# Norms between sub-layers handed on in pieces of 256 columns, and an unread target of squares that orders nothing

## The chip, the core and the metric

The kernel runs on one core of a Trainium2 chip. A core has four engines that compute, each with its own queue of instructions that it works off in order: TensorE (PE, matmuls and transposes into PSUM), VectorE (DVE), ScalarE (ACT) and GpSimd (POOL). A further one, SyncE (SP), issues most DMAs. They meet by semaphores. The metric is the time of one execution in microseconds.

## The reference

A decoder trunk of two layers on 256 tokens of width 1024. Each layer has three sub-layers, and each of these has a root-mean-square norm ahead of it and one behind it, whose output is added to the residual x:

```python
def rms_norm(x, g):
    xf = x.astype(jnp.float32)
    y = xf * lax.rsqrt(jnp.mean(xf * xf, axis=-1, keepdims=True) + RMS_EPS)
    return (y * g.astype(jnp.float32)).astype(x.dtype)
```

The sub-layers are a mix of four token mixers, a cross-attention into 256 memory tokens, and an MLP with squared ReLU of width 4096. All of it is in float32.

## The kernel before, in words

The 256 tokens are two tiles of 128 (t0 and t1), with tokens on partitions. The residual x is kept as two tiles of 128 by 1024. A matmul of float32 quality is made from three (`mm3`): operands are split into a rounded part (hi, cast by ScalarE) and what is left (lo, a VectorE subtraction). Weights are read by DMA into five slots called raw, cast, subtracted and used.

A sub-layer ends with a product of 256 tokens by 1024 (`wide`), which fills two PSUM banks of 512 columns for each token tile, t0 first. Behind it stands a boundary, for each tile the following steps. `post_bank`: ScalarE squares a bank and sums the squares; the squares themselves go to an unread tile named junk; VectorE multiplies the bank by a gain. `post`: GpSimd adds eps to the sum and takes a power, which are two instructions on 128 by 1; VectorE makes the new x from that scale in two halves of 512 columns. `pre`: VectorE multiplies x by the next norm's gain (xg), TensorE transposes xg in two groups of four blocks into banks C, ScalarE copies each group (the rounded part of hT) and VectorE makes the low part. Sums of squares of the new x follow, for a scale that is used later. Where the MLP ends and the next layer's mix begins (`normed`), the scale is needed at once: it is put on a diagonal (g<-ident) and the transposes are matmuls with that diagonal.

The order of instructions on every engine is made at build time by a planner: an operation is ready when what it depends on is planned, ready ones are taken by start time, then rank, then place in the program. Tiles come from pools with few slots (`NB`), PSUM banks from pools A, B, C and S. A pool with one slot makes its users follow one another: the junk tile was such a pool, so that all squares kept the order of the program.

At the start, x is loaded in four DMAs on the queues of SP and ACT, c0 of both tiles and then c1, and `pre_first` scales both tiles on diagonals and fills four banks A with 128-column matmuls, bank by bank for both tiles.

In the trace, L631 is ScalarE's helper, L642, L648 and L654 are VectorE's (L654 GpSimd's too), L676 GpSimd's power, L685 a matmul, L690 a transpose, L728 and L738 DMA issues.

Of the kernel before, what the change touches and what calls it, by code (L numbers as in the profile page):

```python
# [12 lines left out]
BF16 = mybir.dt.bfloat16  # L13
AF = mybir.ActivationFunctionType
OP = mybir.AluOpType
# [4 lines left out]
D = 1024  # L20
T = 256
# [3 lines left out]
C = 64  # L25
RMS_EPS = 1e-6
# [191 lines left out]
def body(nc, tc, wts, x, mem, memT, pc, rows, r256, cmpw, cmpe, relb, lora, cst, out, dbg=None):  # L218
    from contextlib import ExitStack
    with ExitStack() as ctx:  # L220
# [4 lines left out]
        Prog(nc, tc, sb, ps, dr, wts, x, mem, memT, pc, rows, r256, cmpw, cmpe, relb, lora, cst, out, dbg).run()  # L225


NB = {"raw": 5, "hi": 8, "lo": 8, "g8": 7, "g4": 12, "g2": 13, "g1": 5, "junk": 1, "s": 14, "x8": 6,
      "p1": 1, "tok1": 1, "tok2": 1, "lk": 1, "ng": 1}
NPS = {"A": 4, "B": 2, "C": 2, "S": 8}  # L230

# [7 lines left out]
           "sb": ()}  # L239
HOME = {tag: s for s, tags in STRETCH.items() for tag in tags}  # L240
LEAD = 24
KEEP = 1000.0
TICK = 10.24 / 3
WARM = 3060
# [4 lines left out]
class VT:  # L249
# [4 lines left out]
    def __init__(self, name, shape, dtype, tag, dram=False):  # L254
        self.name, self.shape, self.dtype, self.tag, self.dram = name, tuple(shape), dtype, tag, dram
        self.real = None
        self.likes = range(4, 7) if tag == "g8" else ()
# [110 lines left out]
class Sched:  # L368
# [10 lines left out]
    def add(self, eng, cost, outs, ins, emit, cols=0.0):  # L379
        op = Op(eng, cost, [v for v in outs if isinstance(v, V)], [v for v in ins if isinstance(v, V)], emit,  # L380
                self.rank, len(self.ops))
        op.cols = cols
        self.ops.append(op)
        for v in op.ins:
            t = v.t
            for w, box in t.writes:
                if t.psum or meet(box, v.box):
                    self.dep(op, w, LAT[w.eng] if w.eng != eng else OWN[eng])
            t.reads.append((op, v.box))
        for v in op.outs:  # L390
            t = v.t
            for w, box in t.writes:
                if t.psum or meet(box, v.box):
                    self.dep(op, w, 0.0 if w.eng == eng else LAT[w.eng])
            for r, box in t.reads:
                if r is not op and (t.psum or meet(box, v.box)):
                    self.dep(op, r, 0.0 if r.eng == eng else 0.1)
            t.writes.append((op, v.box))
        for v in op.outs + op.ins:
            if not v.t.ops or v.t.ops[-1] is not op:  # L400
                v.t.ops.append(op)
        if eng == "PE" and self.after is not None:
# [204 lines left out]
class Prog:  # L607
# [226 lines left out]
    def setup(self):  # L834
        self.pct = self.keep([128, DEPTH, NPC], "pct")
        self.warm_up()
        xr = self.x.rearrange("o (t p) d -> p (o t) d", p=128)
        self.xt = [self.keep([128, D], "x%d" % t) for t in range(2)]
        for c in range(2):
            for t, eng in enumerate((self.nc.sync, self.nc.scalar)):  # L840
                cs = slice(512 * c, 512 * c + 512)
                self.dma(self.xt[t][:, cs], xr[:, t, cs], eng=eng)
        self.dma(self.pct, self.pc)
        self.ident = self.keep([128, 128], "ident")
        self.s.add("POOL", 0.5, [self.ident], [], lambda: make_identity(self.nc, real(self.ident)))
        self.mhalf = self.keep([128, 8], "mhalf")
        self.memset(self.mhalf, -0.5)

    def warm_up(self):
# [71 lines left out]
    def sumsq(self, src_list):  # L921

        acc = self.small(2)
        for i, s in enumerate(src_list):
            j = self.tile([128, 512], "junk", BF16)
            self.act(j, s, AF.Square, scale=D ** -0.5, accum=acc[:, i:i + 1])
        return acc

# [6 lines left out]
    def to_hT_half(self, t, q, src, hT, scale=None):  # L935


        hh, hl = hT
        p = self.bank("C", (128, 4, 128))
        for j in range(4):  # L940
# [5 lines left out]
        self.split(hh[:, 4 * q:4 * q + 4, s], hl[:, 4 * q:4 * q + 4, s], p)  # L946
# [8 lines left out]
    def pre(self, t, g, hT, normed, out):  # L955


        x = self.xt[t]
        xg = self.tile([128, D], "g4")
        H2 = (slice(0, 512), slice(512, 1024))  # L960

        def stat():
            return self.rstd(self.sumsq([x[:, :512], x[:, 512:]]))

        for s in H2:
            self.tt(xg[:, s], x[:, s], g[:, s], OP.mult)
        scale = None
        if normed:
            scale = self.tile([128, 128], "g1")
            self.ts(scale, self.ident, stat())  # L970
        for q in range(2):
            self.to_hT_half(t, q, xg[:, 512 * q:512 * q + 512], hT, scale)
        if normed is False:
            out[t] = stat()
        elif normed is None:
# [4 lines left out]
            out[t] = e  # L980

    def pre_first(self, hT):
        dg = []
        for t, x in enumerate(self.xt):
            if t == 0:
                acc = self.sumsq([x[:, :512], x[:, 512:]])
            else:
                acc = self.small(2)
                sq = self.tile([128, 512], "g2")
                self.stt(sq, x[:, :512], 1.0 / D, x[:, :512], OP.mult, OP.mult)  # L990
                self.red(acc[:, 0:1], sq, OP.add)
                j = self.tile([128, 512], "junk", BF16)
                self.act(j, x[:, 512:], AF.Square, scale=D ** -0.5, accum=acc[:, 1:2])
            dg.append(self.tile([128, 128], "g1"))
            self.ts(dg[-1], self.ident, self.rstd(acc))
        for q in range(4):
            p = self.bank("A", (128, 2, T))
            for t in range(2):
                for k in range(2):
                    i = 128 * (2 * q + k)  # L1000
                    self.mm(p[:, k, 128 * t:128 * t + 128], self.xt[t][:, i:i + 128], dg[t])
            for k in range(2):
                self.split(hT[0][:, 2 * q + k], hT[1][:, 2 * q + k], p[:, k], self.pcol(0, "g_pre", 1, 2 * q + k))

    def post_bank(self, st, i, bank, g, cs=None):

        if not st:
            st.extend((self.small(4), self.tile([128, D], "g4")))
        acc, yg = st
        cs = cs or slice(512 * i, 512 * i + 512)  # L1010
        j = self.tile([128, 512], "junk", BF16)[:, :cs.stop - cs.start]
# [3 lines left out]
    def post(self, t, st, eps, out=None, after=None):  # L1015

        acc, yg = st
        a, b = acc if isinstance(acc, tuple) else (acc[:, 0:1], acc[:, 1:2])
# [3 lines left out]
        x = self.xt[t]  # L1022
        for i in range(2):
            cs = slice(512 * i, 512 * i + 512)
            op = self.stt(x[:, cs], yg[:, cs], rr, x[:, cs], OP.mult, OP.add)
            if after is not None:
                self.s.dep(op, after, -9.0)
            if out is not None:
                self.dma(out[:, cs], x[:, cs])

    def boundary(self, t, st, eps, gpre, hT, normed, rs):
        self.post(t, st, eps)
        self.pre(t, gpre, hT, normed, rs)

    def at(self, rank, f, *args):
# [5 lines left out]
    def wide(self, l, names, act, gpost, done):  # L1041

        banks = [[self.bank("A") for _ in range(2)] for _ in range(2)]
        ah, al = act
        for half in range(2):
            ks = range(4 * half, 4 * half + 4)
            us = []
            for t in range(2):
# [5 lines left out]
                for k, c in order:  # L1054
# [643 lines left out]
    def mix(self, l, hT):  # L1698
# [69 lines left out]
        self.hT, self.rs = xT, {}  # L1768

        def done(t, st):  # L1770
            self.at(0, self.boundary, t, st, 4 * D * RMS_EPS, gpre, xT, False, self.rs)

        self.wide(l, [("mo", k) for k in range(8)], mT, gpost, done)
        self.dump("x_mix", self.xt)
# [75 lines left out]
    def xattn(self, l):  # L1850
# [384 lines left out]
```

## Time and profile before

| what | value |
|---|---|
| median of 3 runs | 1087.66 us (1087.47 to 1088.67) |
| the profiled execution, its own time | 1090.18 us |
| its span in the trace | 1088.1 us |
| TensorE busy | 1069.9 us |
| VectorE, ScalarE, GpSimd busy | 856.8, 657.5, 96.1 us |

The rows below come from the page's first section and from two views of the trace: the table of stretches, which gives for each engine its busy time in a stretch, and the timeline, which gives the start, the time and the form of instructions on one engine, with the idle time ahead of them and what ended it in brackets.

### The profile page before, as it was taken

The page shows a single profiled execution, that of the slowest core. Times are in us where ns is not written, and L with a number is a line of the kernel's source. Part 1 is how long each engine was busy: PE and PEld are TensorE (multiplying, and loading weights), DVE is VectorE, ACT ScalarE, POOL GpSimd, SP SyncE. Part 2 cuts the span into 40 slices and gives each one's busy share as a digit, 9 for nine tenths or more (in the row PEclk, how much of TensorE's full clock was granted, in tenths as well). Part 3 has the DMA queues.
Part 4 walks back from the last instruction along what each step waited for, and adds up shares of the span by engine and source line. Part 5 has one row for each costly group of instructions (what it writes and reads, how often), then busy time and mean ns, then how long its engine had stood idle before and what let it go on. Part 6 is the DMA issues. An engine that isn't in the chain of part 4 may idle for free.

```text
span 1088.1 us, 20208 instructions
## 1 busy us (share of the span) xinstructions
PE 1069.9 (98%) x7848; PEld 936.1 (86%) x7848; DVE 856.8 (79%) x1347; ACT 657.5 (60%) x1069; POOL 96.1 (9%) x154
## 2 busy tenths in 40 slices
PE   8999999999999999999999999999999999999997
PEld 7989877888998899999889998778888987999996
DVE  6867887866767689888796767977867667999997
ACT  7574655645555667776665664644546455776673
POOL 2000011001100110000020000100002002000000
PEclk9999999999999999999999999999999999999999
DMA  8546555755546699998945257356645467889981
GB/s 328 164 128 183 210 174 165 266 186 169 170 157 218 212 273 288 267 279 254 298 165 172 79 160 254 126 174 201 237 164 173 149 224 210 255 267 293 270 265 51
DMA packets 75970, 225.18 MB, mean 207 GB/s; under 512 B 12223, under 2 KB 14015, under 8 KB 75748
## 3 DMA queue, kind: packets, MB, share of 16 engines
q1 hardware_dynamic: 71268, 207.65, 55.7%
q0 software_dynamic: 4320, 15.73, 8.8%
q8 instruction: 61, 1.00, 0.4%
q10 hardware_dynamic: 288, 0.52, 0.2%
q14 instruction: 33, 0.27, 0.1%
HBM read 221.77 MB, written 3.15 MB: 207 GB/s over the span
## 4 chain that ended last, share of the span: by engine, by line
PE 88%; DMA 3%; DVE 3%; issue 2%; ACT 2%; POOL 2%; SPq 0%; POOLq 0%; DVEq 0%; ACTq 0%
PE A L685 47%; PE C L685 18%; PE S L685 12%; PE B L685 8%; DMA g<-wts 2%; PE C L690 2%; DVE g L642 1%; POOL s L654 1%; DMA raw<-wts 1%; ACT junk L631 1%; DVE lo L642 1%; DVE x L648 1%; ACT g L631 1%; PE B L690 0%; POOL s L676 0%
## 5 line engine op out<-in xcount | busy, mean ns | idle before, releaser
L642 DVE TENSOR_TENSOR lo<-raw,hi 128x1024 fp32r<-128x1024 f32 (+1 forms) x308 | 368.4, 1213 | 70.2 <-ACT hi L631 41.8
L631 ACT ACTIVATE hi<-raw 128x1024 fp32r<-128x1024 f32 (+1 forms) x308 | 316.2, 1049 | 136.7 <-PE A L685 67.1
L685 PE MATMUL A<-hi,g 128*128 128x512 f32 (+2 forms) x1152 | 370.3, 389 | 0.9 <-ACT g L631 0.5
L685 PEld LDWEIGHTS A<-hi,g 128*128 128x128 f32 x1152 | 214.5, 188 | 48.1 <-issue 4.3
L685 PE MATMUL A<-lo,g 128*128 128x512 f32 (+2 forms) x576 | 220.2, 382 | 0.0
L642 DVE TENSOR_TENSOR g<-g,g 128x512 f32<-128x512 f32 (+3 forms) x218 | 187.9, 886 | 9.8 <-ACT g L631 8.5
L631 ACT ACTIVATE g<-g 128x512 fp32r<-128x512 f32 (+7 forms) x228 | 149.0, 693 | 43.3 <-DVE g L642 19.6
L685 PE MATMUL A<-g,hi 128*128 128x256 f32 x928 | 169.2, 285 | 0.0
L685 PE MATMUL C<-g,hi 128*128 128x256 f32 x960 | 167.7, 278 | 1.1 <-ACT g L631 1.1
L685 PEld LDWEIGHTS C<-g,hi 128*128 128x128 f32 x960 | 147.4, 188 | 3.7 <-ACT g L631 1.5
L685 PEld LDWEIGHTS A<-g,hi 128*128 128x128 f32 x928 | 141.2, 188 | 5.2 <-issue 3.4
L685 PE MATMUL C<-g,lo 128*128 128x256 f32 x480 | 133.5, 278 | 0.0
L685 PE MATMUL A<-g,lo 128*128 128x256 f32 x464 | 129.1, 278 | 0.0
L631 ACT ACTIVATE g<-C 128x512 fp32r<-128x512 f32 (+5 forms) x119 | 59.4, 513 | 110.8 <-PE C L685 84.6
L685 PEld LDWEIGHTS A<-lo,g 128*128 128x128 f32 x576 | 108.4, 188 | 17.5
L685 PE MATMUL S<-g,g 128*128 128x512 f32 x450 | 108.3, 391 | 0.3 <-DVE g L642 0.3
L685 PEld LDWEIGHTS S<-g,g 128*128 128x128 f32 x450 | 84.3, 188 | 19.0 <-DVE g L642 0.8
L685 PEld LDWEIGHTS C<-g,lo 128*128 128x128 f32 x480 | 91.0, 190 | 0.0
L685 PEld LDWEIGHTS A<-g,lo 128*128 128x128 f32 x464 | 87.3, 188 | 0.2 <-DVE lo L642 0.2
L631 ACT ACTIVATE g<-A 128x512 f32<-128x512 f32 (+3 forms) x70 | 39.5, 567 | 54.4 <-PE A L685 42.3
L654 POOL TENSOR_SCALAR s<-s 128x1 f32<-128x1 f32 (+1 forms) x38 | 27.3, 719 | 349.8 <-ACT junk L631 297.1
L642 DVE TENSOR_TENSOR g<-C,g 128x512 fp32r<-128x512 f32 (+3 forms) x66 | 37.0, 587 | 23.7 <-ACT g L631 17.3
(144 smaller groups left out, 1079.0 us busy)
## 6 DMA issues: line engine op xcount, KB each, us to landing
raw<-wts SPq DMA_DIRECT2D x300, 512.0 KB, 4.7
g<-wts SPq DMA_DIRECT2D x90, 256.0 KB, 5.3
g<-wts POOLq DMA_DIRECT2D x30, 512.0 KB, 5.7
g<-rows SPq DMA_DIRECT2D x11, 512.0 KB, 4.7
g<-memT SPq DMA_DIRECT2D x12, 256.0 KB, 6.9
g<-cmpw SPq DMA_DIRECT2D x4, 512.0 KB, 4.5
raw<-wts SPq DMA_DIRECT2D x4, 498.0 KB, 6.2
raw<-wts SPq DMA_DIRECT2D x4, 480.0 KB, 6.2
```

Of the source, the lines that this page charges most:

```text
L631: e = lambda: self.nc.scalar.activation(real(out), real(in_), func, bias=real(bias), scale=real(scale), accum_out=real(accum))
L642: f = lambda: e.tensor_tensor(real(out), real(a), real(b), op)
L648: f = lambda: self.nc.vector.scalar_tensor_tensor(real(out), real(a), real(s), real(b), op0=op0, op1=op1)
L654: f = lambda: e.tensor_scalar(real(out), real(a), real(s1), real(s2), op0=op0, **kw)
L685: e = lambda: self.nc.tensor.matmul(real(out), real(lhsT), real(rhs), start=start, stop=stop, skip_group_check=True)
L690: self.pe(0.109, out, [in_, self.ident], lambda: self.nc.tensor.transpose(real(out), real(in_), real(self.ident)), 128)
```

## The change

The junk tile is kept for the whole program, and writes to it make no dependencies (`sink`). At boundaries that aren't `normed`, the new x, xg and the transposes come in pieces of 256, 256 and 512 columns (`PIECES`), `post_bank` and the boundary have rank -1, and the squares of the new x rank 3. The two halves of x of t0 are loaded first, one by each queue, and `pre_first` makes all matmuls of t0 before those of t1.

```diff
-NB = {"raw": 5, "hi": 8, "lo": 8, "g8": 7, "g4": 12, "g2": 13, "g1": 5, "junk": 1, "s": 14, "x8": 6,
+NB = {"raw": 5, "hi": 8, "lo": 8, "g8": 7, "g4": 12, "g2": 13, "g1": 5, "s": 14, "x8": 6,
...
+PIECES = ((0, 2), (2, 2), (4, 4))
...
         for v in op.outs:
             t = v.t
+            if t.sink:
+                continue
...
-        for c in range(2):
-            for t, eng in enumerate((self.nc.sync, self.nc.scalar)):
+        for t in range(2):
+            for c, eng in enumerate((self.nc.sync, self.nc.scalar)):
...
+        self.junk = self.keep([128, 512], "junk", BF16)
+        self.junk.t.sink = True
...
+        for k, n in PIECES:
+            s = slice(128 * k, 128 * (k + n))
+            self.x_new(t, s)
+            self.tt(xg[:, s], x[:, s], g[:, s], OP.mult)
+            self.to_hT(t, k, n, xg[:, s], hT)
+        old = self.rank(3)
         if normed is False:
-            out[t] = stat()
+            out[t] = self.rstd(self.sumsq([x[:, :512], x[:, 512:]]))
...
-        for q in range(4):
-            p = self.bank("A", (128, 2, T))
-            for t in range(2):
+        ps = [self.bank("A", (128, 2, T)) for _ in range(4)]
+        for t in range(2):
+            for q, p in enumerate(ps):
                 for k in range(2):
...
-                        self.post_bank(st, c, banks[t][c], gpost)
+                        self.at(-1, self.post_bank, st, c, banks[t][c], gpost)
...
-            self.at(0, self.boundary, t, st, D * RMS_EPS, gpre, hT, None, self.rs)
+            self.at(-1, self.boundary, t, st, D * RMS_EPS, gpre, hT, None, self.rs)
```

The planner turns this into other orders. At the fourth boundary (cross-attention to MLP, layer 1), TensorE had the eight transposes of t0 (C from xg and ident) in two groups, three matmuls ahead of the end of t1's second bank (A_10267); then came the MLP's first bank (A_10425):

```order
5338 L685 MATMUL A_10267<-hi_10175,g_1916_10000 128x512
5339 L685 MATMUL A_10267<-lo_10241,g_1916_10000 128x512
5340 L685 MATMUL A_10267<-hi_10175,g_1917_10018 128x512
5341 L690 MATMUL C_10388<-ident,g_1976_10374 128x128 x4
5342 L690 MATMUL C_10397<-ident,g_1976_10374 128x128 x4
5343 L685 MATMUL A_10267<-hi_10237,g_1916_10000 128x512
5344 L685 MATMUL A_10267<-lo_10250,g_1916_10000 128x512
5345 L685 MATMUL A_10267<-hi_10237,g_1917_10018 128x512
5346 L685 MATMUL A_10425<-hi_10274,g_1940_10411 128x512
```

After the change (line numbers are five higher, the bank is A_10259 and the MLP's A_10405):

```order
5343 L695 MATMUL C_10369<-ident,g_1941_10362 128x128 x2
5344 L690 MATMUL A_10259<-hi_10170,g_1883_10010 128x512
5345 L690 MATMUL A_10259<-lo_10233,g_1883_10010 128x512
5346 L690 MATMUL A_10259<-hi_10170,g_1884_10018 128x512
5347 L695 MATMUL C_10381<-ident,g_1941_10362 128x128 x2
5348 L690 MATMUL A_10259<-hi_10229,g_1883_10010 128x512
5349 L690 MATMUL A_10259<-lo_10242,g_1883_10010 128x512
5350 L690 MATMUL A_10259<-hi_10229,g_1884_10018 128x512
5351 L695 MATMUL C_10399<-ident,g_1941_10362 128x128 x4
5352 L690 MATMUL A_10405<-hi_10266,g_1907_10377 128x512
```

The transposes are now in groups of two, two and four, the first of them six matmuls ahead of the bank's end. The first group of t1 stands 18 matmuls behind the last of t0; before, it was 27.

At the same boundary, ScalarE had the squares of t0's banks (A_10196 the second), then those of x and two casts of weights (hi), the two copies of transposes (g from C), and only then the squares of t1's banks (A_10263 and A_10267):

```order
736 L631 ACTIVATE junk_10346,s_10330<-A_10196 128x512
737 L631 ACTIVATE junk_10368,s_10369<-x_86 128x512
738 L631 ACTIVATE hi_10378<-raw_10261 128x1024
739 L631 ACTIVATE junk_10384,s_10369<-x_86 128x512
740 L631 ACTIVATE hi_10395<-raw_10286 128x1024
741 L631 ACTIVATE g_1940_10411<-C_10388 128x4x128
742 L631 ACTIVATE g_1940_10411<-C_10397 128x4x128
743 L631 ACTIVATE junk_10417,s_10418<-A_10263 128x512
744 L631 ACTIVATE hi_10422<-raw_10298 128x1024
745 L631 ACTIVATE junk_10436,s_10418<-A_10267 128x512
```

After the change:

```order
737 L636 ACTIVATE junk,s_10316<-A_10188 128x512
738 L636 ACTIVATE junk,s_10357<-A_10255 128x512
739 L636 ACTIVATE junk,s_10366<-x_86 128x512 x2
740 L636 ACTIVATE g_1907_10377<-C_10369 128x2x128
741 L636 ACTIVATE hi_10386<-raw_10253 128x1024
742 L636 ACTIVATE g_1907_10377<-C_10381 128x2x128
743 L636 ACTIVATE junk,s_10357<-A_10259 128x512
744 L636 ACTIVATE g_1907_10377<-C_10399 128x4x128
```

The square of t1's first bank went ahead of those of x, and that of its second stands between copies, with one cast in front of it instead of three. On GpSimd a DMA issue changed places with the pair that makes t0's scale there: it stood ahead of the pair, and now stands behind it.

At the boundary from MLP to mix in layer 0, GpSimd had the pairs (sum and power) in the order t0's post scale (s_1200), t0's diagonal scale (s_1207), t1's post scale (s_1217), t1's diagonal scale (s_1224):

```order
82 L654 TENSOR_SCALAR s_1199_6457<-s_1194_6431,s_813_4360 128x1
83 L676 TENSOR_TENSOR s_1200_6459<-s_1199_6457,mhalf_90 128x1
84 L654 TENSOR_SCALAR s_1206_6486<-s_1203_6471 128x1
85 L676 TENSOR_TENSOR s_1207_6490<-s_1206_6486,mhalf_90 128x1
86 L654 TENSOR_SCALAR s_1216_6514<-s_1211_6495,s_827_4499 128x1
87 L676 TENSOR_TENSOR s_1217_6518<-s_1216_6514,mhalf_90 128x1
```

After the change these are s_1179, s_1192, s_1184:

```order
82 L659 TENSOR_SCALAR s_1178_6456<-s_1175_6424,s_797_4351 128x1
83 L681 TENSOR_TENSOR s_1179_6458<-s_1178_6456,mhalf_90 128x1
84 L659 TENSOR_SCALAR s_1191_6480<-s_1188_6454,s_808_4464 128x1
85 L681 TENSOR_TENSOR s_1192_6482<-s_1191_6480,mhalf_90 128x1
86 L659 TENSOR_SCALAR s_1183_6495<-s_1182_6485 128x1
87 L681 TENSOR_TENSOR s_1184_6498<-s_1183_6495,mhalf_90 128x1
```

The post scale of t1 now stands ahead of t0's diagonal scale. On VectorE the first half of t1's new x stands ahead of t0's diagonal too, and a subtraction of weights ahead of t0's new x. TensorE has 16 weight matmuls of the next layer ahead of t0's diagonal and 6 between the two tiles, where there were 12 and 12.

## Rows read from the trace of the kernel before

**Rows 1.** The page, first section: busy time, share and instructions of each engine.

```profile
PE 1069.9 (98%) x7848; PEld 936.1 (86%) x7848; DVE 856.8 (79%) x1347; ACT 657.5 (60%) x1069; POOL 96.1 (9%) x154
```

**Rows 2.** Table of stretches: length, busy times, clock, DMA share, GB/s.

```profile
400.00:450.00 50.00, 48.89 (x322) 44.22 (x321) 46.01 (x64) 37.96 (x51) 4.32 (x5) 1.00 0.94 270
900.00:950.00 50.00, 47.65 (x284) 40.68 (x283) 43.08 (x63) 35.17 (x63) 9.35 (x12) 1.00 0.77 222
```

**Rows 3.** Timeline (start, us, instruction, wait), TensorE, first and second boundary.

```profile
275.38 0.66 PE L690 MATMUL C<-ident,g 128*128 128x128 f32 x4 [0.22 <-DVE g L642]
...
379.40 0.66 PE L690 MATMUL C<-ident,g 128*128 128x128 f32 x4 [0.21 <-DVE g L642]
```

**Rows 4.** Timeline, TensorE, fourth boundary.

```profile
906.50 0.39 PE L685 MATMUL A<-hi,g 128*128 128x512 f32 x1
907.37 1.26 PE L690 MATMUL C<-ident,g 128*128 128x128 f32 x8 [0.47 <-DVE g L642]
...
909.78 0.51 PE L685 MATMUL A<-hi,g 128*128 128x512 f32 x1 [0.47 <-ACT g L631]
...
910.91 0.74 PE L685 MATMUL A<-hi,g 128*128 128x512 f32 x2 [0.40 <-DVE g L642]
...
917.24 1.50 PE L690 MATMUL C<-ident,g 128*128 128x128 f32 x11 [1.01 <-DVE g L642]
```

**Rows 5.** Timeline, ScalarE, fourth boundary.

```profile
902.72 0.20 ACT L631 ACTIVATION_READ_ACCUMULATOR junk<-A 128x1 f32 x1
...
909.16 1.06 ACT L631 ACTIVATE g<-C 128x512 fp32r<-128x512 f32 x2
...
911.63 0.59 ACT L631 ACTIVATE junk<-A 128x512 bf16<-128x512 f32 x1
```

**Rows 6.** Timeline, GpSimd, fourth boundary.

```profile
903.16 0.95 POOL L738 DMA_DIRECT2D g<-wts  x1 [63.71 <-DMA g<-wts]
...
904.57 0.57 POOL L676 TENSOR_TENSOR s<-s,mhalf 128x1 f32<-128x1 f32 x1
...
912.40 1.39 POOL L654 TENSOR_SCALAR s<-s 128x1 f32<-128x1 f32 x1 [2.30 <-ACT junk L631]
```

**Rows 7.** Timeline, VectorE, fourth boundary.

```profile
905.17 1.42 DVE L648 SCALAR_TENSOR_TENSOR x<-g,s,x 128x512 f32<-128x512 f32 x2 [1.53 <-POOL s L676]
...
910.18 1.27 DVE L642 TENSOR_TENSOR g<-C,g 128x512 fp32r<-128x512 f32 x2
911.38 2.34 DVE L642 TENSOR_TENSOR lo<-raw,hi 128x1024 fp32r<-128x1024 f32 x2
914.48 1.41 DVE L648 SCALAR_TENSOR_TENSOR x<-g,s,x 128x512 f32<-128x512 f32 x2 [0.76 <-POOL s L676]
```

**Rows 8.** Timeline, GpSimd, first boundary.

```profile
262.90 0.30 POOL L654 TENSOR_SCALAR s<-s 128x1 f32<-128x1 f32 x1 [55.43 <-ACT junk L631]
```

**Rows 9.** Timeline, TensorE and ScalarE, start of the program.

```profile
8.29 0.94 PE L685 MATMUL A<-g,x 128*128 128x128 f32 x6 [1.63 <-DVE g L654]
...
6.12 0.63 ACT L631 ACTIVATE junk<-x 128x512 bf16<-128x512 f32 x1 [0.54 <-DMA x<-x]
```

**Rows 10.** Timeline, TensorE, from MLP to mix, layer 0.

```profile
552.44 5.34 PE L685 MATMUL B<-g,raw 128*128 128x256 f32 x24
557.62 2.03 PE L685 MATMUL C<-g,g 128*128 128x128 f32 x16
...
566.17 2.05 PE L685 MATMUL C<-g,g 128*128 128x128 f32 x16 [1.34 <-DVE g L654]
```

**Rows 11.** Timeline, TensorE and ScalarE, MLP of layer 0.

```profile
403.75 1.98 PE L685 MATMUL S<-g,g 128*128 128x512 f32 x8
406.84 0.50 PE L685 MATMUL C<-g,hi 128*128 128x256 f32 x2 [1.11 <-ACT g L631]
...
402.51 2.85 ACT L631 ACTIVATE g<-g 128x1024 fp32r<-128x1024 f32 x3 [4.76 <-DMA g<-wts]
...
406.21 0.57 ACT L631 ACTIVATE g<-C 128x512 f32<-128x512 f32 x1
```

More of the change, by code (lines that the diff above doesn't have):

```diff
@@ L256, in __init__ @@
         self.real = None
+        self.sink = False
         self.likes = range(4, 7) if tag == "g8" else ()
@@ L924, in sumsq @@
         for i, s in enumerate(src_list):
-            j = self.tile([128, 512], "junk", BF16)
+            j = self.junk
             self.act(j, s, AF.Square, scale=D ** -0.5, accum=acc[:, i:i + 1])
@@ L935, in to_hT_half, with to_hT @@
     def to_hT_half(self, t, q, src, hT, scale=None):
+        self.to_hT(t, 4 * q, 4, src, hT, scale)
+    def to_hT(self, t, k, n, src, hT, scale=None):
         hh, hl = hT
-        p = self.bank("C", (128, 4, 128))
-        for j in range(4):
+        p = self.bank("C", (128, n, 128))
+        for j in range(n):
             if scale is None:
@@ L945, in to_hT_half @@
         s = slice(t * 128, t * 128 + 128)
-        self.split(hh[:, 4 * q:4 * q + 4, s], hl[:, 4 * q:4 * q + 4, s], p)
+        self.split(hh[:, k:k + n, s], hl[:, k:k + n, s], p)
     def new_hT(self, still=False):
@@ L959, in pre @@
         xg = self.tile([128, D], "g4")
[L960 to L966, printed above, removed]
         scale = None
         if normed:
+            for s in (slice(0, 512), slice(512, 1024)):
+                self.tt(xg[:, s], x[:, s], g[:, s], OP.mult)
             scale = self.tile([128, 128], "g1")
-            self.ts(scale, self.ident, stat())
-        for q in range(2):
-            self.to_hT_half(t, q, xg[:, 512 * q:512 * q + 512], hT, scale)
+            self.ts(scale, self.ident, self.rstd(self.sumsq([x[:, :512], x[:, 512:]])))
+            for q in range(2):
+                self.to_hT_half(t, q, xg[:, 512 * q:512 * q + 512], hT, scale)
+            return
+        for k, n in PIECES:
+            s = slice(128 * k, 128 * (k + n))
+            self.x_new(t, s)
+            self.tt(xg[:, s], x[:, s], g[:, s], OP.mult)
+            self.to_hT(t, k, n, xg[:, s], hT)
+        old = self.rank(3)
         if normed is False:
-            out[t] = stat()
-        elif normed is None:
+            out[t] = self.rstd(self.sumsq([x[:, :512], x[:, 512:]]))
+        else:
             ss = self.sumsq([x[:, :512], x[:, 512:]])
@@ L980, in pre @@
             out[t] = e
+        self.rank(old)
     def pre_first(self, hT):
@@ L991, in pre_first @@
                 self.red(acc[:, 0:1], sq, OP.add)
-                j = self.tile([128, 512], "junk", BF16)
+                j = self.junk
                 self.act(j, x[:, 512:], AF.Square, scale=D ** -0.5, accum=acc[:, 1:2])
@@ L1001, in pre_first @@
                     self.mm(p[:, k, 128 * t:128 * t + 128], self.xt[t][:, i:i + 128], dg[t])
+        for q, p in enumerate(ps):
             for k in range(2):
@@ L1010, in post_bank, with post_scale @@
         cs = cs or slice(512 * i, 512 * i + 512)
-        j = self.tile([128, 512], "junk", BF16)[:, :cs.stop - cs.start]
+        j = self.junk[:, :cs.stop - cs.start]
         self.act(j, bank, AF.Square, accum=acc[:, i:i + 1])
         self.stt(yg[:, cs], bank, 32.0, g[:, cs], OP.mult, OP.mult)
-    def post(self, t, st, eps, out=None, after=None):
-        acc, yg = st
-        a, b = acc if isinstance(acc, tuple) else (acc[:, 0:1], acc[:, 1:2])
+    def post_scale(self, st, eps):
+        a, b = st[0] if isinstance(st[0], tuple) else (st[0][:, 0:1], st[0][:, 1:2])
         v, rr = self.small(1), self.small(1)
@@ L1021, in post @@
         self.rpow(rr, v)
-        x = self.xt[t]
+        return rr
+    def post(self, t, st, eps, out=None, after=None):
+        self.step = st[1], self.post_scale(st, eps)
         for i in range(2):
             cs = slice(512 * i, 512 * i + 512)
-            op = self.stt(x[:, cs], yg[:, cs], rr, x[:, cs], OP.mult, OP.add)
+            op = self.x_new(t, cs)
             if after is not None:
@@ L1028, in post, with x_new @@
             if out is not None:
-                self.dma(out[:, cs], x[:, cs])
+                self.dma(out[:, cs], self.xt[t][:, cs])
+    def x_new(self, t, cs):
+        yg, rr = self.step
+        x = self.xt[t]
+        return self.stt(x[:, cs], yg[:, cs], rr, x[:, cs], OP.mult, OP.add)
     def boundary(self, t, st, eps, gpre, hT, normed, rs):
-        self.post(t, st, eps)
+        if normed:
+            self.post(t, st, eps)
+        else:
+            self.step = st[1], self.post_scale(st, eps)
         self.pre(t, gpre, hT, normed, rs)
@@ L1770, in done @@
         def done(t, st):
-            self.at(0, self.boundary, t, st, 4 * D * RMS_EPS, gpre, xT, False, self.rs)
+            self.at(-1, self.boundary, t, st, 4 * D * RMS_EPS, gpre, xT, False, self.rs)
         self.wide(l, [("mo", k) for k in range(8)], mT, gpost, done)
```

## The prediction

> **What bounds the kernel now.** I read four views in this order. The page's table of engines has TensorE busy for 1069.9 of 1088.1 us [rows 1], so the most that any new order of the same work can give back is what TensorE stands idle, about 18 us, half of it at the two ends of the program. The table of 50 us stretches says where the rest lies; the two that matter most here idle 1.11 us (400 to 450) and 2.35 (900 to 950), at a granted clock of 1.00, the 2.4 GHz level [rows 2]. The timeline of TensorE then shows each gap and what ended it, and the timelines of the other engines show the chain behind it. The gap list matters more here than busy shares: VectorE is busy 79% and ScalarE 60%, yet almost everywhere TensorE has other matmuls to run while they work, and a faster norm is worth nothing there.
>
> Of the four boundaries that the change rewrites, three have a gap. The first and second (mix to cross-attention and cross-attention to MLP of layer 0) lose 0.22 and 0.21 us, each before the second token tile's transposes [rows 3]. The third (mix to cross-attention, layer 1) loses nothing. The fourth (cross-attention to MLP, layer 1) loses 0.47 + 0.47 + 0.40 before and after the first tile's transposes and 1.01 before the second's: 2.35 us, the whole idle time of its stretch [rows 2, 4]. So the change is mostly worth what it is worth at the fourth.
>
> **The fourth boundary, first tile.** ScalarE's read of the last sum ends at 902.92 [rows 5], but GpSimd starts its pair (sum plus eps, then the power) only after a DMA issue that stood in front of it, at 903.16 for 0.95 us, and the power ends at 905.14 [rows 6]; VectorE makes both halves of x from 905.17 (1.42 us) and then xg [rows 7], and TensorE transposes at 907.37 [rows 4]. In the new order that DMA issue stands behind the pair. A pair that nothing disturbs takes 0.30 + 0.57 us and some 0.13 between [rows 6, 8], so x starts near 903.0 + 1.0 = 904.0, 1.15 us earlier. The pieces of 256 columns help less than they seem to: all three pieces of x still run before the first piece of xg, so the first transposes can start near 904.0 + 1.5 (x) + 0.5 (first xg) = 906.0. In TensorE's order they now stand six matmuls ahead of the bank's end instead of three. A 512-column matmul takes a slot of 0.23 us (eight in 1.98, less the 0.39 of the last, over seven [rows 11]); the last one ahead of the transposes began at 906.50 [rows 4], so TensorE was free at 906.73, and comes to them now at 906.73 - 3 x 0.23 = 906.05. The two meet; the 0.47 goes. The other two gaps were ScalarE's copies at 909.16, behind two squares of x and two casts of weights, and VectorE's low parts at 910.18 [rows 4, 5, 7]. After the change copies alternate with the second tile's last matmuls and one cast, not two, stands ahead of them. I take the whole 1.34 us; if one copy still stands behind a cast, 0.5 of it stays.
>
> **The fourth boundary, second tile.** Here the freed target of the squares matters. Before, both bank squares of the second tile stood behind the first tile's squares of x, though its first bank, which TensorE fills ahead of the second, was full earlier; the second square started at 911.63, the pair began at 912.40, and x at 914.48 [rows 5 to 7]. Now one square goes ahead of x and the last directly behind the bank: bank full near 906.05 + 6 x 0.23 + 4 x 0.12 + 0.2 = 908.1 (0.12 a transpose, from 16 of its size in 2.03 us [rows 10]), square and read 0.7, pair 1.0, x by 256 columns 0.8, xg 0.5, a copy of the first tile's low part between them 0.6, which makes 911.7. TensorE reaches these transposes after 18 further matmuls, 908.3 + 18 x 0.23 = 912.4. The 1.01 goes with 0.7 us to spare. Together -2.35 us; bounds 0 to -2.35.
>
> The pair's first step is what this margin hangs on. Undisturbed it took 0.30 us; at 912.40 it took 1.39, and it ended just behind two VectorE subtractions with both operands in SBUF, which ran 911.38 to 913.72 [rows 6 to 8]. In the new order VectorE reads PSUM there, so I take 0.30. Should such a subtraction lie there after all, the cost is 1.1 us and the margin is gone. The Trainium skill (SBUF — State Buffer, Who interferes with whom) says that a VectorE instruction with two SBUF inputs and a GpSimd instruction that reads SBUF exclude each other for a whole instruction; the trace agrees (0.30 against 1.39). By that rule x and xg, which also read SBUF twice, would hold up GpSimd too, and the second tile's pair would come up to 0.4 us later than I have it: the sum would not change while the 0.7 of margin lasts.
>
> **Boundaries one to three.** The same steps move there, and the two gaps of 0.22 and 0.21 should go: -0.43. The third has nothing to give. In all four TensorE is now asked for the second tile's first piece 18 (512-column) or 36 (256-column) matmuls after the first tile's last, 4.1 us, where before it was further off: the cover is shorter. Each of the eight passes splits its transposes into three groups instead of two. A change between transposes and matmuls shows no idle time of its own where nothing waits, and I take 0.1 us for all eight; a full 0.1 for each would be 0.8. The casts' low parts are pushed behind the pieces, by up to 4 us; TensorE uses them several units later, so I take nothing, with what it costs if that cover is gone under the rivals.
>
> **The start.** The first diagonal matmul waits 1.63 us for a scale on VectorE [rows 9]. The first tile's second half landed at 6.12, behind the other tile's first half; now both halves come first, so the second square follows the first at 5.6 and the scale is ready 0.4 us sooner. But all 16 matmuls of one tile now precede those of the other, so the first bank is full no earlier than before, and one more subtraction of weights, 1.2 us (two in 2.34 [rows 7]), stands ahead of VectorE's first low part. I keep -0.2, with bounds +0.3 and -0.6.
>
> **MLP to mix, layer 0.** Only the unread target changes there, but the order does too. GpSimd made the first tile's diagonal scale before the second tile's post scale, now after it, and VectorE's first x of the second tile stands ahead of the diagonal. TensorE meets the first diagonal 16 weight matmuls (0.43 us each: 24 records between 552.44 and 557.62, two a matmul) after 552.44, at 559.3, where it was 557.62 [rows 10]. I work the diagonal out to 560.7: an added subtraction (1.2) lets x, and with it the second tile's post square, end near 558.6, and two pairs of 1.0 each follow. That is a new wait of 1.4 us. The old wait of 1.34 before the second diagonal shrinks to 0.2, since that tile's x is 2 us earlier. Net +0.25, bounds -1.3 and +1.5.
>
> **MLP, layer 0.** The 1.11 us at 406.84 was a PSUM bank that ScalarE copied at 406.21, behind three casts that had waited for a weight load until 402.51 [rows 11]. In the new order the copy stands ahead of such casts. That could return 1.1 us, but DMA is busy 94% there [rows 2], and a load that comes late stops TensorE elsewhere. I take 0; bounds -1.1 and +1.
>
> **Sum**: -2.35 - 0.43 + 0.1 - 0.2 + 0.25 + 0 = -2.63 us. The profiled execution took 1090.18 us, 2.5 over the median; the differences are taken to hold for both, so 1087.66 - 2.63 = **1085.0 us**.
>
> **Rivals.** (a) *The weight stream takes it back.* With DMA at 94% in MLP 0 the gains of the start and the first two boundaries become a wait for weights, and a part of the fourth's becomes one in the last MLP. For it: the 402.51 load. Against: TensorE has one gap in that stretch, not many. It would leave 0 to 1.5 of the gain: 1086.9. (b) *The diagonal in MLP to mix* waits 1.4 and the second one keeps its 1.34, because VectorE's low parts and subtractions stand ahead of it: -2.63 + 1.14, so 1086.2. (c) *The second tile is late at every boundary*, the side that is slower than before. If a cast (1.05) stands before the last bank square and a subtraction holds GpSimd (1.1), xg is 2.2 us later than worked out, 1.5 over the margin of 0.7. Boundaries one to four then wait 1.5 each, where they waited 0.22, 0.21, 0 and 1.01: +4.6 against -1.34 + 0.1 + 0.05, so 1091.0; the sign turns at a wait of 0.7 each. Against it: the row order of ScalarE has the square ahead of that cast. (d) *The first piece is no sooner, and the change doesn't do what it says*: the pieces gain nothing since x comes whole before xg; what is gained is the squares' and the moved DMA's. This alters no sum, it is my reading already. (e) *The copy in MLP 0 is really free*: -1.1 more, 1083.9.
>
> **Chances.** Forecast 0.5, (a) 0.2, (b) 0.13, (c) 0.07, (e) 0.1. Within 0.2%, which is about what can be told from no change, means 1085.5 to 1089.8. The forecast's own spread is about 0.7, so a quarter of it lies there: faster 0.375 + 0.1 = 0.47, same 0.125 + 0.2 + 0.13 + 0.01 = 0.46, slower 0.07. The range takes in (e), (a) and (b): 1083.6 to 1087.9.
>
> **What would show it.** Right: no gap of TensorE from 904 to 918, GpSimd's pair of the first tile directly behind the read, gaps of a few tenths at most in the first two boundaries. A gap of about 1.4 before the first diagonal in MLP to mix and a small one before the second. Wrong: waits of TensorE for xg in any boundary above 0.3 us, GpSimd steps above 1 us in the second tile's chain, or new waits for weights in either MLP.

## The result, and the profile after

The changed kernel takes 1082.4 us (median of 4 runs, 1081.8 to 1083.2) against 1087.6 before: a ratio of 0.9949, with a 95% interval of 0.9936 to 0.9962. It was timed again in two further sets, at 0.9957 (0.9941 to 0.9973) and 0.9956 (0.9943 to 0.9968). So it is faster by 4 to 5 us. The forecast was 1085.0 with a range that began at 1083.6: the sign was right, the forecast gain about half of the measured one.

The page of the changed kernel, busy times of the engines:

```profile
PE 1068.3 (99%) x7848; PEld 936.8 (87%) x7848; DVE 860.8 (80%) x1371; ACT 660.5 (61%) x1077; POOL 99.3 (9%) x154
```

The span is 1080.3 us where it was 1088.1. TensorE's list of waits (total, times, longest) has shrunk to five:

```profile
PE C L690 <- DVE g L659: 1.2, 1, 1.2
PE C L863 <- DVE g L860: 1.2, 1, 1.2
PE A L690 <- DVE g L659: 0.7, 1, 0.7
PE A L690 <- DVE g L653: 0.7, 1, 0.7
PE B L695 <- DVE g L647: 0.2, 1, 0.2
```

None of them stands at a boundary that the change rewrote; where [rows 3, 4] had waits of TensorE, the changed kernel has none. The fourth boundary after the change, engine by engine (start, time, instruction, wait), first ScalarE's read of the first tile's sum and GpSimd:

```profile
898.54 0.19 ACT L636 ACTIVATION_READ_ACCUMULATOR junk<-A 128x1 f32 x1
...
898.83 0.31 POOL L659 TENSOR_SCALAR s<-s 128x1 f32<-128x1 f32 x1 [63.66 <-ACT junk L636]
899.22 0.57 POOL L681 TENSOR_TENSOR s<-s,mhalf 128x1 f32<-128x1 f32 x1
900.24 0.95 POOL L743 DMA_DIRECT2D g<-wts  x1 [0.45 <-issue]
...
905.15 0.29 POOL L659 TENSOR_SCALAR s<-s 128x1 f32<-128x1 f32 x1 [1.39 <-ACT junk L636]
```

VectorE:

```profile
899.83 1.54 DVE L653 SCALAR_TENSOR_TENSOR x<-g,s,x 128x256 f32<-128x256 f32 x3 [0.37 <-POOL s L681]
901.39 1.36 DVE L647 TENSOR_TENSOR g<-x,g 128x256 f32<-128x256 f32 x3
...
905.10 0.68 DVE L653 SCALAR_TENSOR_TENSOR g<-A,g 128x512 f32<-128x512 f32 x1
...
906.29 0.87 DVE L653 SCALAR_TENSOR_TENSOR x<-g,s,x 128x256 f32<-128x256 f32 x2
907.08 0.76 DVE L647 TENSOR_TENSOR g<-x,g 128x256 f32<-128x256 f32 x2
```

TensorE:

```profile
901.87 0.44 PE L695 MATMUL C<-ident,g 128*128 128x128 f32 x2
...
908.34 0.60 PE L695 MATMUL C<-ident,g 128*128 128x128 f32 x4
```

GpSimd's pair follows ScalarE's read at once, the DMA issue comes behind it, and the steps of 0.31, 0.57 and 0.29 us are the undisturbed ones, where the second tile's first step had been 1.39 [rows 6]. TensorE transposes at 901.87 and 908.34 and waits for neither; the second tile's xg was ready at 907.84, half a microsecond ahead.

### The profile page after: what moved, and what is told of

The parts are those of the page before. It is cut to its first block, busy times and chain, and to the rows that moved or that the text cites. A ratio compares the mean times of both kernels' runs of the same rounds, so it can differ in the third digit from the quotient of the medians.

```text
span 1080.3 us, 20196 instructions
## 1 busy us (share of the span) xinstructions
PE 1068.3 (99%) x7848; PEld 936.8 (87%) x7848; DVE 860.8 (80%) x1371; ACT 660.5 (61%) x1077; POOL 99.3 (9%) x154
## 4 chain that ended last, share of the span: by engine, by line
PE 97%; DVE 1%; DMA 1%; POOL 1%; issue 0%; ACT 0%; SPq 0%; DVEq 0%; POOLq 0%; ACTq 0%
PE A L690 51%; PE C L690 20%; PE S L690 14%; PE B L690 9%; PE C L695 2%; DMA raw<-wts 1%; PE B L695 1%; POOL s L659 0%; DVE g L647 0%; DVE g L653 0%; SPq L733 0%; POOL s L681 0%; ACT hi L636 0%; DVE x L653 0%; ACT junk L636 0%
```

## Where the time went, by two traces of each kernel

The first traces of the two kernels are 7.75 us apart in span, the medians only 5.2. The kernel of before was therefore traced a second time, and so was the changed one.

> The kernel of before, unchanged, for a second trace of it. Its first profiled execution took 2.6 us more than its median, the changed kernel's 0.7. Theory V (the first trace shows waits that are not in every execution, so comparing the two traces overstates the gain by about 2 us): span 1085 to 1086.5 and one or more of the gaps at 331, 406, 543 and 676 us shorter by half or gone. Rival W (the waits are fixed by the order, the 2.6 us lie in single long steps elsewhere or outside the span): the same 14 gaps within 0.1 us each, 8.7 to 9.1 us in sum.

> The changed kernel, unchanged, timed beside the others, with a second trace of it. 1081.8 to 1083.2 as before; under V gaps of 2 to 4 us in sum that do not all stand where the first trace has them, under W the same four (0.68, 0.65, 1.23, 0.21).

The medians were 1087.2 (before) and 1083.0 (after), the second spans 1084.0 and 1079.7. In its second trace the kernel of before waits for fewer things:

```profile
PE C L685 <- DVE g L654: 1.3, 1, 1.3
PE C L690 <- DVE g L642: 1.2, 2, 1.0
PE A L685 <- DVE g L654: 1.2, 1, 1.2
PE C L856 <- DVE g L853: 1.2, 1, 1.2
PE C L685 <- ACT g L631: 0.5, 1, 0.5
PE A L685 <- ACT g L631: 0.5, 1, 0.5
PE A L685 <- DVE g L642: 0.4, 1, 0.4
```

The waits at 331, 379, 543 and 676 us, and the first of the four at the fourth boundary, are gone; that in MLP 0 is 0.50 instead of 1.11; leaving out the one of 1.2 at 1.18 us, before the first matmuls of the program, all waits sum to 5.3 us where the first trace had 8.9. So theory V holds, though the span is below its range. Of the changed kernel's waits three of four came again (0.74, 0.60 and 1.22), as W had it. The first of the four at the fourth boundary went because the DMA issue ahead of GpSimd's pair, 0.24 us behind the end of ScalarE's read in the first trace [rows 5, 6], began 0.48 ahead of it in the second, and x came 1.5 us behind that read instead of 2.25. At 331 us a late load is the cause: a cast on ScalarE waited for weights in the first trace of before, a copy of transposes and VectorE's work on it stood behind that cast, and TensorE then waited 0.84 us,

```profile
329.21 1.06 ACT L631 ACTIVATE hi<-raw 128x1024 fp32r<-128x1024 f32 x1 [1.95 <-DMA raw<-wts]
...
331.79 0.44 PE L690 MATMUL C<-ident,g 128*128 128x128 f32 x2 [0.84 <-DVE g L654]
```

while in the second the same cast ran at once:

```profile
327.34 1.06 ACT L631 ACTIVATE hi<-raw 128x1024 fp32r<-128x1024 f32 x1
```

The same program meets late loads in one execution and not in the next. The following table follows TensorE's instructions in order of start (there are 7848 in each kernel) and gives when one starts, against the first trace of before:

| behind (instruction number) | before, 2nd | after, 1st | after, 2nd | after, 2nd less before, 2nd, since the row above |
|---|---|---|---|---|
| start (1200) | +0.15 | +0.30 | +0.11 | -0.04 |
| first boundary (2400) | +0.19 | +0.12 | -0.05 | -0.20 |
| second boundary (3020) | -0.82 | -1.12 | -1.29 | -0.23 |
| begin of MLP 0 (3200) | -1.25 | -2.31 | -2.48 | -0.76 |
| MLP to mix (4300) | -1.91 | -3.12 | -3.30 | -0.16 |
| ahead of the fourth boundary (6600) | -3.25 | -4.04 | -4.62 | +0.02 |
| behind it (7200) | -4.07 | -7.78 | -8.37 | -2.93 |
| end of the span | -4.06 | -7.75 | -8.34 | +0.02 |

Two places make 3.7 of the 4.3 us: the fourth boundary and the begin of MLP 0. The other rows are too small to be told: in two traces of one program (the changed kernel with the old start, below) the stretch from instruction 1200 to 2400 differs by 0.9 us and that from 3200 to 4300 by 1.2. The two places stand clear of this. From instruction 3020 to 3200 (MLP 0) each of seven traces with freed squares and three pieces takes 25.48 us, and the three traces with before's boundaries and squares 26.25, 26.67 and 30.15; from 6600 to 7200 (fourth boundary) the same seven take 100.9 to 101.2 and the three 103.8 to 104.7.

**The fourth boundary: a wait costs more than its figure.** The second trace of before has three waits there, 1.88 us in sum:

```profile
904.84 0.40 PE L685 MATMUL A<-hi,g 128*128 128x512 f32 x1
905.70 0.50 PE L685 MATMUL A<-hi,g 128*128 128x512 f32 x1 [0.46 <-ACT g L631]
906.04 0.39 PE L685 MATMUL A<-lo,g 128*128 128x512 f32 x1
906.83 0.73 PE L685 MATMUL A<-hi,g 128*128 128x512 f32 x2 [0.40 <-DVE g L642]
...
911.75 0.39 PE L685 MATMUL A<-hi,g 128*128 128x512 f32 x1
913.16 1.60 PE L690 MATMUL C<-ident,g 128*128 128x128 f32 x12 [1.02 <-DVE g L642]
```

A 512-column matmul starts 0.227 us behind the one before it when nothing waits. From 904.84 to 905.70 it took 0.86: 0.63 lost, and the row says 0.46, because it counts idle time from the modelled end of the last matmul (0.39 or 0.40 long), which a following matmul would have overlapped by 0.16. The next step, 905.70 to 906.04, is again 0.11 longer than 0.227. Counted from start to start, the three waits cost 0.63 + 0.56 + 1.19 = 2.38, and 0.11 follows each of the first two: 2.6, and with smaller ones 2.9, which is what the table has. In the first trace the four waits of [rows 4], 2.35 by their figures, cost 0.64 + 0.64 + 0.56 + 1.18 = 3.0 from start to start, and 3.2 with the longer step behind two of them; the table has 3.7 there.

**MLP 0: a copy behind casts that wait for weights.** The order of ScalarE there is that of [rows 11] in three traces with before's boundaries, and TensorE's wait in them goes with the moment at which the load arrives. The two not yet shown, ScalarE and TensorE, first the second trace of before, then a kernel that has only the new start:

```profile
401.08 2.85 ACT L631 ACTIVATE g<-g 128x1024 fp32r<-128x1024 f32 x3 [4.05 <-DMA g<-wts]
404.78 0.57 ACT L631 ACTIVATE g<-C 128x512 f32<-128x512 f32 x1
...
405.41 0.50 PE L685 MATMUL C<-g,hi 128*128 128x256 f32 x2 [0.50 <-ACT g L631]
```

```profile
403.41 2.85 ACT L631 ACTIVATE g<-g 128x1024 fp32r<-128x1024 f32 x3 [6.46 <-DMA g<-wts]
407.11 0.57 ACT L631 ACTIVATE g<-C 128x512 f32<-128x512 f32 x1
...
407.73 0.80 PE L685 MATMUL C<-g,hi 128*128 128x256 f32 x2 [2.90 <-ACT g L631]
```

Loads at 401.08, 402.51 and 403.41 give waits of 0.50, 1.11 and 2.90 us. In the changed kernel the cast waits for a load until 402.93, and TensorE does not:

```profile
399.87 0.60 ACT L636 ACTIVATE g<-C 128x512 f32<-128x512 f32 x1 [1.81 <-PE C L690]
...
402.93 1.37 ACT L636 ACTIVATE g<-g 128x1024 fp32r<-128x1024 f32 x2 [1.31 <-DMA g<-wts]
...
404.45 0.40 PE L690 MATMUL C<-g,hi 128*128 128x256 f32 x2
```

The copy that frees the PSUM bank now stands ahead of the casts (399.87), so a late load reaches nobody. By the stretches above that is worth 0.8 and 1.2 us against the two traces of before, and 4.7 against the kernel with the new start alone, whose load came last.

## Experiments: which part does it

Each kernel is the changed one, or that of before, with one part taken back or done alone. Ratios are against runs of before in the same set. [rows 4] is the picture of before at the fourth boundary.

**The freed squares alone** (kernel of before):

```diff
...
+            if t.sink:
+                continue
...
-            j = self.tile([128, 512], "junk", BF16)
+            j = self.junk
...
```

> Kernel of before, and of the change only the unread target of the squares that makes no dependencies; halves of 512 columns, ranks and start as before. Theory S (most of the gain is the freed order of the squares: t1's chain at the fourth boundary, the bank copy in MLP 0, the waits between): TensorE's gap before t1's transposes at the fourth boundary is gone and the one of 1.11 us in MLP 0 too, the gaps around t0's transposes there stay at 0.3 to 0.5 each since the DMA issue still stands ahead of GpSimd's pair; time 1084.0 to 1085.0. Rival P (the pieces and ranks carry it): all gaps of the fourth boundary stay, 1086.8 to 1087.6.

Measured 1086.9 us, ratio 0.9995 (0.9981 to 1.0008). The time is one that P gave, and no gain can be told; but P's other sign, that all waits of the fourth boundary stay, did not come. At the fourth boundary the second tile's transposes no longer wait (910.39), but the matmuls behind the first tile's, which need their copies and low parts, still do:

```profile
905.81 0.50 PE L688 MATMUL A<-hi,g 128*128 128x512 f32 x1 [0.38 <-ACT g L634]
907.19 0.73 PE L688 MATMUL A<-hi,g 128*128 128x512 f32 x2 [0.64 <-DVE g L645]
910.39 0.63 PE L693 MATMUL C<-ident,g 128*128 128x128 f32 x4
```

and MLP 0 still has its wait (0.64 with the load at 401.25). The runs spread from 1083.8 to 1090.6.

**All but the freed squares** (changed kernel, the unread target again one slot):

```diff
-NB = {"raw": 5, "hi": 8, "lo": 8, "g8": 7, "g4": 12, "g2": 13, "g1": 5, "s": 14, "x8": 6,
+NB = {"raw": 5, "hi": 8, "lo": 8, "g8": 7, "g4": 12, "g2": 13, "g1": 5, "junk": 1, "s": 14, "x8": 6,
...
-            j = self.junk
+            j = self.tile([128, 512], "junk", BF16)
...
```

> The changed kernel, with the unread target again a pool of one slot, so that squares keep the order of the program; pieces, ranks and start as changed. Theory S: the bank squares of t1 stand again behind the squares of t0's x, TensorE waits for t1's transposes at the fourth boundary (0.3 to 1.0 us), other gaps come back; time 1084.0 to 1085.5. Rival P: 1082.2 to 1083.2, no gap at the fourth boundary.

Measured 1086.9, ratio 0.9993 (0.9981 to 1.0004), slower than either answer. Now the first tile's waits are gone and the second tile's comes back in part; MLP 0 has 1.52:

```profile
910.86 0.77 PE L695 MATMUL C<-ident,g 128*128 128x128 f32 x4 [0.27 <-DVE g L647]
...
406.84 0.50 PE L690 MATMUL C<-g,hi 128*128 128x256 f32 x2 [1.52 <-ACT g L636]
```

Theory S said that the squares carry the gain, P that the pieces do. Both fall: the time of neither alone can be told from before's (the intervals leave room for 2 us), together they give 5 us. They remove different waits of the same boundary, and there each gives its part: from instruction 6600 to 7200 the freed squares alone are 0.7 us shorter than the second trace of before, the pieces alone 1.8, both together 2.9. The wait at the begin of MLP 0 goes with neither alone, and is in no trace of a kernel with both. Why the medians don't show the 0.7 and 1.8 stays open; the traced executions of these two kernels (1085.1 us each) were among their faster ones.

**Two pieces of 512 columns** instead of three:

```diff
-PIECES = ((0, 2), (2, 2), (4, 4))
+PIECES = ((0, 4), (4, 4))
```

> The changed kernel with two pieces of 512 columns at the boundaries in place of 256, 256 and 512; all else as changed. If the size of the pieces matters little (x comes whole before the first xg, as the order shows): 1082.2 to 1083.0, gaps at the fourth boundary of 0.3 us at most. If the pieces carry the gain of the first tile there: TensorE waits 0.4 to 0.5 us before t0's transposes and again for the copies behind them, 1083.5 to 1084.5.

Measured 1085.1, ratio 0.9975 (0.9964 to 0.9987): half the gain, and outside both answers. The idle times around t0's transposes are almost gone (0.06 left), so the order removes most of them whatever the size; counted from start to start 0.6 us stay behind those transposes. There is a new wait a little later, in the MLP, for a bank that ScalarE copies late:

```profile
913.11 0.66 PE L695 MATMUL C<-ident,g 128*128 128x128 f32 x4 [0.69 <-ACT g L636]
```

and a second wait of 1.34 before the second diagonal of MLP to mix, as in before. In MLP 0 the copy stands behind the casts again (at 403.31); TensorE did not wait for it in this trace, in which those casts had their weights in time. The span is 3.0 us longer than that of the changed kernel's second trace: 1.4 at the fourth boundary, 0.4 in MLP 0, and 1.3 in places too small to be told singly. So the pieces matter by the order that they lead to, and not by one first piece that is sooner.

**The old ranks** (boundary 0, squares without a rank of their own):

```diff
-        old = self.rank(3)
...
-                        self.at(-1, self.post_bank, st, c, banks[t][c], gpost)
+                        self.post_bank(st, c, banks[t][c], gpost)
...
-            self.at(-1, self.boundary, t, st, D * RMS_EPS, gpre, hT, None, self.rs)
+            self.at(0, self.boundary, t, st, D * RMS_EPS, gpre, hT, None, self.rs)
```

> The changed kernel with the ranks of before (boundary 0, bank squares without a rank of their own, no rank for the squares of x); pieces, free squares and start as changed. If freed squares and pieces make the gain together: 1082.0 to 1083.2 and no gap above 0.3 us at the fourth boundary. If the ranks are what puts the squares of t1 ahead: a gap of 0.5 to 1.0 us before t1's transposes there, 1083.5 to 1084.5.

Measured 1082.0, ratio 0.9952 (0.9938 to 0.9966), no wait at the fourth boundary. The ranks do nothing that can be told.

**The start.** Three kernels: the new start alone on the kernel of before, the changed kernel with the old start, and the changed kernel with the new loads but the old order of banks. The edit of the second, which has both parts of the old start:

```diff
-        for t in range(2):
-            for c, eng in enumerate((self.nc.sync, self.nc.scalar)):
+        for c in range(2):
+            for t, eng in enumerate((self.nc.sync, self.nc.scalar)):
...
-        ps = [self.bank("A", (128, 2, T)) for _ in range(4)]
-        for t in range(2):
-            for q, p in enumerate(ps):
+        for q in range(4):
+            p = self.bank("A", (128, 2, T))
+            for t in range(2):
...
```

> The kernel of before with the new start alone (loads and first matmuls). If the new start costs time: 1087.0 to 1088.5, not faster than before, TensorE at record 1200 within 0.3 us of the kernel of before or later, and the gaps at the fourth boundary (0.46, 0.40, 1.02) still there. If it gains what my sum gave it: 1086.5 to 1087.0 and 0.2 to 0.6 us earlier at record 1200.

> The changed kernel with the loads of x and the first matmuls in the order of before; all else as changed. Theory L (the second subtraction of weights that the change puts ahead of the first low parts eats the earlier start: in the changed kernel TensorE waits 0.68 and then 0.65 us, and is 0.3 us late at record 1050): one wait of about 1.6 us and no second one, time 1081.9 to 1082.4, 0 to 0.4 below the changed kernel. Rival (the new start gains what its first wait lost, 0.9 us): 1083.0 to 1083.6.

> The changed kernel with the start of before, again, now beside the changed kernel on one chip. If the new start costs time: 1080.0 to 1081.5, 1 to 2 us below the changed kernel of this set, with no wait of TensorE between 11 and 13 us. If the difference between the two sets was one of chips and days: within 0.5 us of it.

> The changed kernel, beside it: 1081.8 to 1083.2, waits of about 0.7 and 0.6 us at 7 and 12 us, 1.2 at 557, none at the fourth boundary.

> The changed kernel with its loads of x, but the first matmuls bank by bank for both tiles as before. The order then has only one subtraction of weights ahead of VectorE's first low parts. Theory L: the first real matmul at about 7.5 us as in the changed kernel and no second wait of 0.65, so 0.6 to 1.0 us below the changed kernel, 1081.4 to 1081.9, unless later stages differ. Rival (the order of the banks has no part in it): the second wait stays and the time is the changed kernel's, 1082.2 to 1082.8.

The new start alone: 1087.4, ratio 1.0001 (0.9991 to 1.0011), and instruction 1200 at +0.13 where the second trace of before has +0.15. No gain can be told. The changed kernel shows why; TensorE and VectorE at the start:

```profile
7.52 3.84 PE L690 MATMUL A<-g,x 128*128 128x128 f32 x32 [0.68 <-DVE g L659]
...
12.12 0.39 PE L690 MATMUL A<-g,hi 128*128 128x256 f32 x1 [0.65 <-DVE g L653]
...
9.21 2.47 DVE L647 TENSOR_TENSOR lo<-raw,hi 128x1024 fp32r<-128x1024 f32 x2 [0.55 <-ACT hi L636]
11.60 1.65 DVE L653 SCALAR_TENSOR_TENSOR g<-A,pct,g 128x256 fp32r<-128x256 f32 x4
```

The first matmuls come at 7.52 instead of 8.29 [rows 9], but two subtractions of weights now stand ahead of VectorE's first low part (11.60), and TensorE waits again at 12.12; by instruction 1200 nothing is left of the 0.77. The kernel with the new start alone has the same two subtractions, and a wait of 0.34 at 11.90. With the old start the changed kernel took 1080.7 in one set, below both answers, and 1081.7 in the other, where the changed kernel beside it took 1082.2; the intervals of the ratios, 0.9937 to 0.9962 and 0.9943 to 0.9968, overlap. So the old start is no worse and perhaps 0.5 us better, which these runs don't settle; the 1 to 2 us that I expected are not there. With the new loads and the old banks TensorE is 1.24 us ahead at instruction 1200, as expected and more, but 1.06 late at 2100, behind the first mix, where it waited 0.72 us for a scale from GpSimd, which no other trace lists; the time is the changed kernel's (1082.3). A gain at the start was not kept.

**Four pieces of 256 columns**, with the old start:

```diff
-PIECES = ((0, 2), (2, 2), (4, 4))
+PIECES = ((0, 2), (2, 2), (4, 2), (6, 2))
```

> The changed kernel with the start of before and four pieces of 256 columns at the boundaries. With no wait left at the four boundaries a finer cut has nothing to take: within 0.5 us of the kernel with the old start. If each group of transposes costs 0.1 us on TensorE as my upper bound had it (eight passes, one group more each): 0.8 us slower than that.

Measured 1084.6, ratio 0.9982 (0.9971 to 0.9993): 2.9 slower than three pieces, more than either answer. The span is 1.6 longer than in the second trace with three pieces and the old start: 0.4 in the stretch of the second boundary, 0.4 in MLP 0 and 0.6 at the fourth, in steps too short for a row of their own. Why, and where the rest goes, stays open.

## Why the prediction was wrong, step by step

Two steps failed: the price of the waits at the fourth boundary was too low, and the wait in MLP 0 was taken as one that nothing would be gained from.

- **Fourth boundary, -2.35**: the mechanism was right in its details. First x 1.1 us behind the read (measured 898.73 to 899.83, it was 902.92 to 905.17 [rows 5, 7]), first transposes without a wait, the second tile with some tenths to spare (0.5, said 0.7), GpSimd's step at 0.29. The size was wrong: 2.9 in the second traces, 3.7 in the first. I added up the printed idle times, and each of these waits costs TensorE 0.16 us more for the overlap that it lost and in most cases 0.11 in its next step. By the start-to-start count of the four waits of [rows 4] the term would have been -3.2, and the forecast 1084.1.
- **MLP 0, taken as 0**: this choice failed. I saw that the copy would stand ahead of the casts, and that the load was late, and then let the DMA share of 94% argue that TensorE would stop elsewhere. It did not: the changed kernel has no wait in that MLP. Rival (e), to which I gave 0.1, is what happened. Rival (a) fell with it: nothing was taken back.
- **First and second boundary, -0.43**: measured -0.20 and -0.23. That the sum agrees is luck: the second trace of before had no wait of 0.21 to lose at the second boundary, and steps of this size can't be told.
- **Start, -0.2**: no gain that can be told (-0.04 between the second traces, 1.0001 in the ratio). The subtraction that I named as a bound stands where TensorE lost it again.
- **MLP to mix, +0.25**: measured -0.16. The first diagonal waits 1.23 (1.4 worked out) and the second no longer does. But the chain was another than mine. The second tile's square was read early, at 551.87; GpSimd then needed 3.42 us for one step of 128 by 1 and held the first diagonal's pair behind it (last section). Rival (b) fell, since VectorE made the second diagonal in time.
- **Passes in more groups, +0.1**: not to be told apart, but four pieces cost more (2.9) than my bound of 0.8, so this term is not understood.
- **The reference, 2.5 us over the median**: I took each wait of one trace as a fixed property of the program. About 3.6 of its 8.9 us were not waited in the next execution of the same program. Two of my terms were built on such waits (0.21 at the second boundary, 0.47 at the fourth).
- **Rival (c)** had a margin of 0.7 us to break and did not: no second tile was late.

The medians move by 4.1 to 5.2 us and the second traces by 4.3. With -3.2 at the fourth boundary and -0.76 at MLP 0 the sum would have given 1083.4; what makes the last 1.0 us down to the median is not known. The 0.8 at MLP 0 depends on the moment of a load, which was seen to move by 2.3 us; that this is also why runs of before spread from 1085.0 to 1091.8 and those of the changed kernel only from 1080.2 to 1083.2 fits, and was not shown by a trace of each run.

## What to carry to other kernels

Count a wait of TensorE from start to start of its matmuls against the spacing without a wait, not by the printed idle time: at 0.4 us of idle the true price was half as much again. Take a second trace of the same program before a sum is built on gaps, since those that a load caused may not be there again; the ones to cut first are those in which a short copy stands in order behind an instruction that waits for a load. And of two changes whose gain can't be told in the time of either alone, both together can show one, where they remove different waits of one chain.

## What the runs showed of the hardware

One GpSimd step on 128 by 1 can last 3.42 us. In the boundary from MLP to mix of the changed kernel:

```profile
551.98 3.42 POOL L659 TENSOR_SCALAR s<-s,s 128x1 f32<-128x1 f32 x1 [0.72 <-ACT junk L636]
...
550.97 1.21 DVE L647 TENSOR_TENSOR lo<-raw,hi 128x1024 fp32r<-128x1024 f32 x1
552.11 1.41 DVE L653 SCALAR_TENSOR_TENSOR x<-g,s,x 128x512 f32<-128x512 f32 x2
553.43 1.28 DVE L647 TENSOR_TENSOR g<-x,g 128x512 f32<-128x512 f32 x2
554.63 0.68 DVE L653 SCALAR_TENSOR_TENSOR g<-g,g 128x512 f32<-128x512 f32 x1
```

It began while VectorE was in a row of instructions that follow one another without a pause, all with two operands in SBUF, and ended at 555.40, 0.09 us behind the last of them (555.31). Undisturbed such a step takes 0.30 [rows 8]. Five further traces with this order, of the changed kernel and of kernels made from it, have the same 3.42, and a wait of 1.2 us before the first diagonal. But the first trace of the changed kernel with the old start, whose second trace is one of the five, has 0.96:

```profile
551.27 0.96 POOL L659 TENSOR_SCALAR s<-s,s 128x1 f32<-128x1 f32 x1 [0.72 <-ACT junk L636]
...
551.39 1.41 DVE L653 SCALAR_TENSOR_TENSOR x<-g,s,x 128x512 f32<-128x512 f32 x2
```

VectorE's row was the same and stood equally far behind GpSimd's start (0.12 us from there to x in both). The step ended 0.08 us behind the first of the two instructions on x, and TensorE did not wait for the first diagonal, which bears out the chain above. So one program can get either; what decides it stays open. The 1.2 us saved were nearly gone at instruction 6600.

The Trainium skill (SBUF — State Buffer, Who interferes with whom) says that such VectorE instructions and a GpSimd one that reads SBUF exclude each other for a whole instruction; the traces agree, as the step ended just behind a VectorE instruction both times, and show that GpSimd got its turn between two of them in one trace and not before the end of the row in six. In the prediction I let this rule reach x and xg with 0.4 us at most; here a row of six such instructions cost 3.1.
